# A hand-written order for the projection stage of an RWKV-7 layer

## The chip, the cores and the metric

The kernel runs on one NeuronCore of a Trainium2 chip. The core has five engines that run their own instruction streams in order: TensorE (PE, the matrix multiplications), VectorE (DVE), ScalarE (ACT), GpSimd (POOL) and SyncE (SP, which here issues every DMA). The metric is the device time of one execution in microseconds; the figure compared is the median over runs. One further execution is recorded by the profiler, and all durations below come from that one.

## The reference, cut to what matters

The model is a trunk of four layers over 512 latent tokens and 256 context tokens of width 1024: convolution, RWKV-7 time mixing, grouped-query attention, convolution. Each layer is modulated by vectors that are computed from a conditioning vector and a weight matrix. The change concerns the features of the second layer:

```python
def rwkv_features(h, proj, with_out):
    xx = centred_shift(h) - h
    lerp = lambda n: h + xx * mu[n]
    k = lerp(2) @ w_k
    v = heads(lerp(3) @ w_v)
    kk = heads(k * k_k)
    kk = kk * lax.rsqrt(jnp.sum(kk * kk, axis=-1, keepdims=True) + 1e-12)
    xw, xa = lerp(1), lerp(4)
    for d in range(2):
        w_log = -jax.nn.softplus(-(w0[d] + jnp.tanh(xw @ w1[d]) @ w2[d])) - 0.5
        a = jax.nn.sigmoid(a0[d] + (xa @ a1[d]) @ a2[d])
        ...  # decay exp(-exp(w_log)), k * (1 + (a - 1) * k_a), a
    r = heads(lerp(0) @ w_r)
    g = lerp(5) @ w_g
```

A recurrence over the tokens (the scan) then uses r, k, v, kk, a and the decay. `modulation(c, mod_w[i], mod_b[i])` is a product of a vector with a 1024 x 3072 matrix; the one of the last layer (i = 3) is computed inside this stage.

## The kernel before, in words

Tokens lie on the free axis, 768 of them with gaps of one between the two streams; channels lie on the 128 partitions in 8 tiles (`NT`). A projection of one column tile is the sum over 8 channel tiles. Each product is made of three matmuls in a split format: high weight by high input, high by low, low by high (`mm3`, L186), for 256 context and 512 latent tokens. These six matmuls are called a chunk here; a column tile has 8 chunks. The tile `pps` (for v `vps`) is a PSUM tile of two banks, and two of them exist.

The stage goes through these parts:

- The ramp (L743 on): for each channel tile m, `norm` (L676) makes the normed input H and the shifted difference XX on DVE and ACT; `mr.step` mixes the input for r (`mq`, then a high part `mh` and a low part `ml`); a low-rank product (`lps`, L746) reads H and XX.
- The r phase: 8 column tiles of `w_r`. Beside it run the low-rank product for the decay (`lora`, L775, on `mt`), the mixed input for the gate, which goes to DRAM (`dgx`), and the modulation of layer 3 (`mps` L205, `mrow`, `mpt` L212).
- The k phase: 8 column tiles of `w_k`, each with a follow-up: on ACT the copy out of PSUM (L834), kp and its square `ksq`; on PE the matmuls `pa` (L845) whose tanh gives the rate `ta`; `kd` and q on DVE; `pn` (L865) sums the squares, ACT copies them to `rn` and POOL takes the power -0.5 (L868); `pr` (L874) spreads that over the channels; kp, `ta` and `kh` are multiplied; `pb` (L887) sums q to `b`. Results go to DRAM as `dF` and `db`.
- The v phase: one column tile of `w_v` (`V_FIRST = 1`) in the stage, the other seven given as a generator to the scan, which places their chunks among its own work.

The first matmul of the scan is `pz` (L1017). It reads `RW`, small weights that are loaded into memory that the stage held before.

In this kernel, a scheduler with a simulated timeline orders the instructions of the stage on each engine; the scan behind it is written in its final order (`manual_schedule`). The modulation is advanced by two steps for every r tile and three for every k tile. Weight columns are loaded two tiles ahead on SP (L164), and ACT and DVE split them into `whi` and `wlo` (L173, L175).

Of the kernel before, what the change touches and what calls it, by code (L numbers as in the profile page):

```python
# [16 lines left out]
D = 1024  # L17
# [61 lines left out]
class Trunk:  # L79
# [582 lines left out]
    def rwkv_features(self, i, c1, cv):  # L662
# [5 lines left out]
        bank = lambda tag, name: ps_x.tile([P, 512], F32, tag=tag, name=name, bufs=2)  # L668
# [6 lines left out]
        def norm(m):  # L675
            for z in (0, CTX + 1, W - 1):  # L676
                nc.gpsimd.memset(H[m][:, z:z + 1], 0.0)
            for s, o, t0, n in segs:
                hs = H[m][:, 1 + o:1 + o + n]
                nc.vector.scalar_tensor_tensor(out=hs, in0=self.xs(m, s), scalar=self.gs[i][:, m, s:s + 1],  # L680
                                               in1=self.R[:, t0:t0 + n], op0=ALU.mult, op1=ALU.mult)
                nc.scalar.activation(hs, hs, AF.Identity, bias=self.shift_c(i, m, s))
            t = self.tp.tile([P, 783], F32, tag="sq", name="nb")
# [15 lines left out]
        def wcol(name, m):  # L699
            return self.wload(I[name][0][:, m * P:(m + 1) * P], NT, P, nc.vector)  # L700

        class Mix:

            def __init__(mx, n):
                mx.n, mx.h, mx.l = n, [], []

            def step(mx):
                k, n = len(mx.h), mx.n
                if k == NT:
                    return  # L710
# [10 lines left out]
        self.mp, self.mbufs = c1.enter_context(tc.tile_pool(name="mp1", bufs=1)), 2  # L721
        self.mod_ps = lambda: (bank("fill", "mps"), lambda: bank("fill", "mpt"))
        mod3 = self.modulation(DEPTH - 1, 256)
# [3 lines left out]
        lsegs = ((0, 0, CTX), (1, CTX + 1, SEQ))  # L727

# [5 lines left out]


        wa = lora_w("rwkv_a1")
        wm = fa.tile([P, NT, P], F32, tag="lw", name="lmu", bufs=2)
        nc.vector.tensor_tensor(out=wm, in0=wa, in1=mu[:, 4 * NT:5 * NT].unsqueeze(2).to_broadcast([P, NT, P]), op=ALU.mult)
        pl = [bank("fill", "lps") for _ in range(2)]
        ahead = [wcol("rwkv_w_r", m) for m in range(2)]  # L740
        for m in range(NT):
            norm(m)
            mr.step()  # L743
            for j, (w, x) in enumerate(((wa, H[m][:, 1:W - 1]), (wm, XX[m]))):
                for b, t0, n in lsegs:
                    nc.tensor.matmul(pl[b][:, :n], w[:, m, :], x[:, t0:t0 + n], start=m == 0 and j == 0, stop=m == NT - 1 and j == 1)  # L746
        for b, (_, t0, n) in zip(pl, psegs):
            nc.scalar.activation(AL[:, t0:t0 + n], b[:, :n], AF.Copy)
        self.rpool.close()
        self.xcpool.close()  # L750
        self.xpool.close()
        fp = c1.enter_context(tc.tile_pool(name="f1", bufs=1))
        self.mark("L1lora")

        def project(ws, x):

            pw = [(self.ps_b.tile([P, 1024], F32, tag="big", name="pps"), w) for w in ws]
            for k in range(NT):
                for ps, w in pw:
                    self.mm3([(ps[:, 0:CTX], slice(0, CTX)), (ps[:, 512:1024], slice(CTX + 1, CTX + 1 + SEQ))],  # L760
                             [a[:, k:k + 1] for a in w], ([x.h[k]], [x.l[k]]), 1, first=k == 0, last=k == NT - 1)
            return [ps for ps, _ in pw]

        def evac(dst, ps, f):
            for o, t0, n in psegs:
                f(dst[:, t0:t0 + n], ps[:, o:o + n], t0, n)

        def lora(n, name, done):

            wr = lora_w(name)  # L770
            ps = [bank("fill", "lps") for _ in range(2)]
            for k in range(NT):
                t = plain(n, k)
                for b, t0, n_ in lsegs:
                    nc.tensor.matmul(ps[b][:, :n_], wr[:, k, :], t[:, t0:t0 + n_], start=k == 0, stop=k == NT - 1)  # L775
                if k == NT - 1:
                    done(ps)
                if k % 2:
                    yield

        def phase(label, name, x, nxt, body, post, ahead):

            self.mark(label)
            done = []
            for m in range(NT):
                if not done:
                    n = 2 if m == 0 else 1
                    done = project([ahead.pop(0) for _ in range(n)], x)
                    for j in range(m + 2, min(m + 2 + n, NT)):
                        ahead.append(wcol(name, j))  # L790
                if m:
                    post(m - 1, prev)
                prev = body(m, done.pop(0))
                for _ in range(2):
                    next(fill, None)
                for _ in range(2 if x is mr else 3):
                    next(mod3, None)
                if nxt is not None:
                    nxt.step()
            return lambda: post(NT - 1, prev)  # L800

        def decay_done(ps):
            for b, (_, t0, n) in zip(ps, psegs):
                nc.scalar.activation(self.T[0][0:64, t0:t0 + n], b[0:64, :n], AF.Tanh)
                nc.scalar.activation(self.T[1][64:128, t0:t0 + n][:, ::-1], b[64:128, :n], AF.Tanh)

        def gate_lerp():

            for k in range(NT):
                nc.sync.dma_start(self.dgx[k], plain(5, k))  # L810
                yield

        def filler():
            yield from lora(1, "rwkv_w1", decay_done)
            yield from gate_lerp()

        fill = filler()

        def r_body(m, ps):
            r = self.tp.tile([P, TOK], F32, tag="t", name="r")  # L820
            evac(r, ps, lambda d, p, t0, n: nc.scalar.activation(d, p, AF.Copy))
            nc.sync.dma_start(self.dF[m][:, 1, :], r)

        last = phase("L1r", "rwkv_w_r", mr, mk, r_body, lambda m, st: None, ahead)
        ahead = [wcol("rwkv_w_k", 0), wcol("rwkv_w_k", 1)]
        A2 = fa.tile([P, NT, P], F32, tag="lw", name="A2", bufs=2)
        nc.sync.dma_start(A2, I["rwkv_a2"][0].rearrange("d l (m c) -> (d l) m c", c=P))


        def k_body(m, ps):  # L830
            r = fp.tile([P, TOK], F32, tag="f3", name="rl")
            nc.sync.dma_start(r, self.dF[m][:, 1, :])
            k = self.tp.tile([P, TOK], F32, tag="t", name="k")
            evac(k, ps, lambda d, p, t0, n: nc.scalar.activation(d, p, AF.Copy))  # L834
            kp = fp.tile([P, TOK], F32, tag="f0", name="kp")
            nc.scalar.activation(kp, k, AF.Copy, scale=self.vec("k_k")[:, m:m + 1])
            sq = self.tp.tile([P, TOK], F32, tag="sq", name="ksq")
            nc.scalar.activation(sq, kp, AF.Square)
            ta, kd = [], []
            for d in range(2):  # L840
                w = slice(64 * d, 64 * d + 64)
                t = fp.tile([P, TOK], F32, tag=f"ta{d}", name=f"ta{d}")
                for o, t0, n in psegs:
                    pa = bank("post", "pa")
                    nc.tensor.matmul(pa[:, :n], A2[w, m, :], AL[w, t0:t0 + n], start=True, stop=True)  # L845
                    nc.scalar.activation(t[:, t0:t0 + n], pa[:, :n], AF.Tanh, scale=0.5,
                                         bias=self.a0h[:, d * NT + m:d * NT + m + 1])
                ta.append(t)
                f = fp.tile([P, TOK], F32, tag="f1", name="kd", bufs=2)
                nc.scalar.activation(f, t, AF.Identity, scale=self.KA[:, 1, m:m + 1], bias=self.KA[:, 0, m:m + 1])  # L850
                nc.vector.tensor_tensor(out=f, in0=f, in1=k, op=ALU.mult)
                for sl, h in ((1, HA), (0, HB)):
                    nc.sync.dma_start(self.dF[m][h, 2 + 2 * d + sl, :], f[h])
                kd.append(f)
            q = fp.tile([P, TOK], F32, tag="f2", name="q")
            nc.vector.tensor_tensor(out=q, in0=kd[0], in1=kd[1], op=ALU.add)
            nc.vector.scalar_tensor_tensor(out=q, in0=q, scalar=self.vec("r_k")[:, m:m + 1], in1=r, op0=ALU.mult, op1=ALU.mult)
            return kp, sq, ta, q
# [1138 lines left out]
```

## Time and profile before

| | us |
|---|---|
| median of 3 runs | 2523.52 (2518.95 to 2536.96) |
| profiled execution | 2515.72 |
| its span, first to last instruction | 2513.9 |
| mean granted TensorE clock, as a share of the full one | 0.934 |
| PE busy over the span | 2317.8 (92%) |
| DVE, ACT, POOL busy | 1420.7, 1107.9, 513.7 |

The stage lies between about 432 and 774 us of the span. Times in the rows are microseconds from the start of the span, unless they are marked ns. The granted clock stands as a share of full speed. "Idle before" is the time that an engine waited in front of an instruction, with what ended the wait. An fp32 matmul shows up as two matmul records; those of the split format as one.

### The profile page before, as it was taken

The page shows a single profiled execution, that of the slowest core. Times are in us where ns is not written, and L with a number is a line of the kernel's source. Part 1 is how long each engine was busy: PE and PEld are TensorE (multiplying, and loading weights), DVE is VectorE, ACT ScalarE, POOL GpSimd, SP SyncE. Part 2 cuts the span into 40 slices and gives each one's busy share as a digit, 9 for nine tenths or more (in the row PEclk, how much of TensorE's full clock was granted, in tenths as well). Part 3 has the DMA queues.
Part 4 walks back from the last instruction along what each step waited for, and adds up shares of the span by engine and source line. Part 5 has one row for each costly group of instructions (what it writes and reads, how often), then busy time and mean ns, then how long its engine had stood idle before and what let it go on. Part 6 is the DMA issues. An engine that isn't in the chain of part 4 may idle for free. (4 is left out here: it accounts for less than half of the span.)

```text
span 2513.9 us, 45763 instructions
## 1 busy us (share of the span) xinstructions
PE 2317.8 (92%) x17983; PEld 1818.0 (72%) x17983; DVE 1420.7 (57%) x2565; ACT 1107.9 (44%) x2642; POOL 513.7 (20%) x600
## 2 busy tenths in 40 slices
PE   7999978999887889999999899989999999989987
PEld 4777757677656667777776677878988989865655
DVE  4856665643533766666664342745455464668774
ACT  4222243333542256666666643446445454442232
POOL 0000002000101123223220004445344454410000
PEclk9999989999888889899887899999999999999999
DMA  8877633267564554444432463111111211215442
GB/s 269 242 218 212 173 101 118 75 190 225 169 197 149 155 124 113 110 120 118 110 89 64 143 219 114 33 53 43 43 58 45 68 60 51 83 31 133 119 127 84
DMA packets 358997, 304.50 MB, mean 121 GB/s; under 512 B 110886, under 2 KB 300414, under 8 KB 358782
## 3 DMA queue, kind: packets, MB, share of 16 engines
q1 hardware_dynamic: 358782, 301.57, 41.5%
q8 instruction: 142, 2.33, 0.4%
q14 instruction: 73, 0.60, 0.1%
HBM read 215.82 MB, written 57.77 MB: 109 GB/s over the span
## 5 line engine op out<-in xcount | busy, mean ns | idle before, releaser
L173 ACT ACTIVATE whi<-wraw 128x1024 fp32r<-128x1024 f32 x168 | 177.0, 1056 | 408.7 <-PE cps L186 180.6
L175 POOL TENSOR_TENSOR wlo<-wraw,whi 128x1024 fp32r<-128x1024 f32 x70 | 168.2, 2406 | 183.0 <-ACT whi L173 170.2
L370 DVE SCALAR_TENSOR_TENSOR Y<-yp,VC,Y 128x783 f32<-128x783 f32 (+1 forms) x224 | 196.8, 891 | 8.1 <-ACT Y L363 4.2
L175 DVE TENSOR_TENSOR wlo<-wraw,whi 128x1024 fp32r<-128x1024 f32 x98 | 120.2, 1228 | 137.8 <-ACT whi L173 129.0
L1750 PE MATMUL pj<-whi,hhi 128*128 128x256 f32 x640 | 182.7, 286 | 5.2 <-ACT junk L1759 3.6
L1750 PE MATMUL pj<-wlo,hhi 128*128 128x256 f32 x640 | 182.2, 285 | 2.4 <-POOL wlo L175 2.4
L1750 PE MATMUL pj<-whi,hlo 128*128 128x256 f32 x640 | 181.9, 285 | 0.0
L186 PE MATMUL cps<-hhi,whi 128*128 128x512 f32 x576 | 178.9, 367 | 3.0 <-ACT hhi L285 3.0
L186 PE MATMUL cps<-hhi,wlo 128*128 128x512 f32 (+1 forms) x576 | 176.9, 361 | 0.0
L186 PE MATMUL cps<-hlo,whi 128*128 128x512 f32 (+1 forms) x576 | 176.5, 360 | 0.0
L186 PEld LDWEIGHTS cps<-hhi,whi 128*128 128x128 f32 x576 | 96.5, 190 | 47.4 <-issue 15.9
L1750 PEld LDWEIGHTS pj<-whi,hhi 128*128 128x128 f32 x640 | 123.7, 193 | 6.5 <-ACT junk L1759 4.2
L186 PE MATMUL ops<-hhi,whi 128*128 128x512 f32 (+1 forms) x320 | 104.9, 370 | 24.6 <-ACT hhi L445 22.2
L1750 PEld LDWEIGHTS pj<-wlo,hhi 128*128 128x128 f32 x640 | 123.9, 194 | 3.3 <-POOL wlo L175 2.6
L1750 PEld LDWEIGHTS pj<-whi,hlo 128*128 128x128 f32 x640 | 123.5, 193 | 0.1
L994 ACT ACTIVATE VT<-c 64x64 f32<-64x64 f32 x384 | 83.5, 218 | 82.9 <-PE c L1269 76.5
L1283 ACT ACTIVATE VT<-o,DC 64x64 f32<-64x64 f32 x352 | 108.8, 309 | 21.5 <-PE o L1278 12.7
L186 PEld LDWEIGHTS cps<-hhi,wlo 128*128 128x128 f32 x576 | 95.9, 189 | 25.9 <-issue 10.0
L186 PEld LDWEIGHTS cps<-hlo,whi 128*128 128x128 f32 x576 | 96.7, 190 | 22.7 <-issue 5.0
L1175 DVE TENSOR_TENSOR Ti<-Ti,tm 96x31 f32<-96x31 f32 (+15 forms) x248 | 105.8, 427 | 6.1 <-POOL tm L1172 0.2
L186 PE MATMUL ops<-hhi,wlo 128*128 128x512 f32 (+1 forms) x320 | 106.5, 363 | 3.0 <-POOL wlo L175 2.2
L186 PE MATMUL ops<-hlo,whi 128*128 128x512 f32 (+1 forms) x320 | 104.9, 356 | 0.5 <-DVE hlo L656 0.5
(343 smaller groups left out, 5806.1 us busy)
## 6 DMA issues: line engine op xcount, KB each, us to landing
mraw<-in_mod_w_dram SPq DMA_DIRECT2D x36, 1024.0 KB
wraw<-in_conv_w_in_dram SPq DMA_DIRECT2D x48, 512.0 KB
wraw<-in_attn_w_in_dram SPq DMA_DIRECT2D x48, 512.0 KB
X<-yp SPq DMA_DIRECT2D x128, 99.4 KB
mraw<-in_mod_w_dram SPq DMA_DIRECT2D x24, 512.0 KB
KR<-dF SPq DMA_DIRECT2D x24, 384.0 KB
F<-dF SPq DMA_DIRECT2D x24, 384.0 KB
X<-yp SPq DMA_DIRECT2D x128, 65.5 KB
```

Of the source, the lines that this page charges most:

```text
L173: nc.scalar.activation(hi[:, :n], raw[:, :n], AF.Copy)
L175: lo_eng.tensor_tensor(out=lo[:, :n], in0=raw[:, :n], in1=hi.bitcast(F32)[:, :n], op=ALU.subtract)
L186: nc.tensor.matmul(ps, a[:, k, m0:m0 + m], b[k0 + k][:, ts], start=first and k == 0 and i == 0, stop=last and k == kt - 1 and i == 2)
L370: taps.append(lambda v=v: nc.vector.scalar_tensor_tensor(out=Y[m], in0=y[:, PE_TAPS + v:PE_TAPS + v + nout], scalar=self.vec("dw", nv)[:, ...
L994: nc.scalar.activation(out, in_, AF.Copy)
L1175: eng("ia", j).tensor_tensor(out=Ti[0:96, j + 1:32, 0:c], in0=Ti[0:96, j + 1:32, 0:c], in1=o, op=ALU.add)
L1283: nc.scalar.activation(G["VT", h2][own, d, q2, hc(hd)], pS[own], AF.Copy, scale=dc[own])
L1750: nc.tensor.matmul(o[:, n, :], a, b[:, k, :], start=kh == 0 and k == 0 and e == 0 and n == 0, stop=kh == 1 and k == 3 and e == 2 and n == 1)
```

## The change

The stage is put under `manual_schedule`, so that PE, DVE, ACT and POOL run its instructions nearly in the order in which the code makes them; SP is still ordered by the scheduler. Column tiles go in pairs, the second 4 chunks behind the first (2 in the first pair of r). A small calendar (`at`, `tick`) places each piece of a key tile's follow-up a set number of chunks behind the tile's last chunk: rate at 0 and 1, norms at 2, kd at 3, the bonus at 4, spread and products at 5, the weighing at 6. The r chunks start inside the ramp. Of the 37 turns of the modulation, 28 come in the r phase and 9 in the k phase. Four PSUM banks are one pool for all helpers, in place of two pools of two. `kp` has two buffers, `b` moves to another buffer, and the rates of even tiles use buffers of the v phase.

```diff
-        bank = lambda tag, name: ps_x.tile([P, 512], F32, tag=tag, name=name, bufs=2)
+        bank = lambda name: ps_x.tile([P, 512], F32, tag="post", name=name, bufs=4)
...
+        def at(d, f):
+            plan.setdefault(now[0] + d, []).append(f)
+
+        def tick():
+            for f in plan.pop(now[0], []):
+                f()
+            now[0] += 1
...
+        def ready(j):
+            if j < len(cols):
+                ws[j] = self.wsplit(raws.pop(j), NT, P, nc.vector)
+                fetch(j + 2)
...
+            at(0, key)
+            at(0, lambda: rate(*psegs[0]))
+            at(1, lambda: rate(*psegs[1]))
+            at(2, norms)
+            at(3, lambda: kd(0))
+            at(3, lambda: kd(1))
+            at(4, bonus)
+            at(5, spread)
+            at(5, products)
+            at(6, weigh)
+
+        def phase(label, j0, x, nxt, body, beside, lead=lambda p: 4, before=lambda k: None):
+            self.mark(label)
+            for p in range(0, NT, 2):
+                ps, L = [big("pps") for _ in range(2)], lead(p)
+                steps = [(e, k) for u in range(NT + L) for e, k in ((0, u), (1, u - L)) if 0 <= k < NT]
+                for u, (e, k) in enumerate(steps):
+                    if e == 0 and p == 0:
+                        before(k + 1)
+                    chunk(ps[e], ws[j0 + p + e], x, k)
+                    if k == NT - 1:
+                        body(p + e, ps[e])
+                        at(0, lambda j=j0 + p + e + 2: ready(j))
+                    if p == NT - 2 and e == 1:
+                        nxt.step()
+                    beside(p // 2, u)
+                    tick()
+            nxt.step()
+
+        with ExitStack() as man:
+            man.enter_context(tc.manual_schedule(engines={nc.tensor.engine, nc.vector.engine, nc.scalar.engine, nc.gpsimd.engine}))
+            fetch(0)
+            fetch(1)
+            wa = lora_w("rwkv_a1")
+            wm = fa.tile([P, NT, P], F32, tag="lw", name="lmu", bufs=2)
+            ready(0)
+            nc.vector.tensor_tensor(out=wm, in0=wa, in1=mu[:, 4 * NT:5 * NT].unsqueeze(2).to_broadcast([P, NT, P]), op=ALU.mult)
...
+            def r_beside(p, u):
+                if u % 2 and (p or u > 7):
+                    next(mod3, None)
+                if p in (1, 2):
+                    if u % 2 == 0:
+                        next(decay, None)
+                    if u % 4 == 3:
+                        next(gate, None)
+
+            phase("L1r", 0, mr, mk, r_body, r_beside, lambda p: 4 if p else 2, ramp)
...
+            phase("L1k", NT, mk, mv, k_body, lambda p, u: next(mod3, None) if p < 3 and u in (6, 9, 12) else None)
...
+            for m in range(V_FIRST):
+                for _ in v_tile(m):
+                    tick()
+            while plan:
+                tick()
```

What this does to the instruction streams is shown at three places. The first is PE at the end of the stage, in front of the scan's first matmul `pz`. Before, behind the last of 24 v chunks:

```order
L186 MATMUL vps<-mh,wlo 128x512
L887 MATMUL pb<-q,C 128x512
L845 MATMUL pa<-AL,A_4453 128x256
L845 MATMUL pa<-AL,A_4453 128x512
L845 MATMUL pa<-AL,A_4453 128x256
L845 MATMUL pa<-AL,A_4453 128x512
L865 MATMUL pn<-blk_3529,ksq 128x2 x6
L874 MATMUL pr<-C,rn 64x128 x12
L887 MATMUL pb<-q,C 128x256
L887 MATMUL pb<-q,C 128x512
```

The same eight rows from `pa` to `pb` follow once more, for the last key tile, and then `pz`. In the changed kernel, the end of the last follow-up on PE:

```order
L891 MATMUL pr<-C,rn 64x128 x12
L186 MATMUL vps<-mh,whi 128x256
L186 MATMUL vps<-mh,whi 128x512
L186 MATMUL vps<-ml,whi 128x256
L186 MATMUL vps<-ml,whi 128x512
L186 MATMUL vps<-mh,wlo 128x256
L186 MATMUL vps<-mh,wlo 128x512
L909 MATMUL pb<-q,C 128x256
L909 MATMUL pb<-q,C 128x512
L186 MATMUL vps<-mh,whi 128x256
```

The follow-ups of the last two key tiles moved in front of the v chunks: behind the last `pb` now come 86 matmuls of v (14.3 chunks) and then `pz`. In both kernels 24 v chunks precede `pz`.

The second place is PE in the k phase, around the rates (`pa`) of a key tile. Before, the four matmuls of the rates of the fifth tile and its norms (`pn`) stand together, ahead of the first v chunk:

```order
L887 MATMUL pb<-q,C 128x512
L845 MATMUL pa<-AL,A_4453 128x256
L845 MATMUL pa<-AL,A_4453 128x512
L845 MATMUL pa<-AL,A_4453 128x256
L845 MATMUL pa<-AL,A_4453 128x512
L865 MATMUL pn<-blk_3529,ksq 128x2 x6
L186 MATMUL vps<-mh,whi 128x256
L186 MATMUL vps<-mh,whi 128x512
```

In the changed kernel, where the second tile of a pair has ended:

```order
L891 MATMUL pr<-C,rn 64x128 x12
L857 MATMUL pa<-AL,A_4532 128x256 x2
L186 MATMUL pps<-mh,whi 128x256
L186 MATMUL pps<-mh,whi 128x512
L186 MATMUL pps<-ml,whi 128x256
L186 MATMUL pps<-ml,whi 128x512
L186 MATMUL pps<-mh,wlo 128x256
L186 MATMUL pps<-mh,wlo 128x512
L909 MATMUL pb<-q,C 128x256
L909 MATMUL pb<-q,C 128x512
L857 MATMUL pa<-AL,A_4532 128x512 x2
```

The rates are split: the 256-wide ones come right at the tile's end, the 512-wide ones a chunk later, and the first tile's spread (`pr`) and weighing (`pb`) stand ahead of each; the norms follow another chunk later.

The third place is DVE at the start of the ramp. Before, with the 512-wide multiplies of all eight tiles ahead of the reciprocal for the context tokens (rows of the first three tiles left out):

```order
L680 SCALAR_TENSOR_TENSOR H_3557<-xl_86,gs_72,R 128x512
L680 SCALAR_TENSOR_TENSOR H_3558<-xl_87,gs_72,R 128x512
L680 SCALAR_TENSOR_TENSOR H_3559<-xl_88,gs_72,R 128x512
L680 SCALAR_TENSOR_TENSOR H_3560<-xl_89,gs_72,R 128x512
L680 SCALAR_TENSOR_TENSOR H_3561<-xl_90,gs_72,R 128x512
L260 RECIPROCAL R<-R 128x256
L175 TENSOR_TENSOR wlo<-wraw,whi 128x1024 x2
```

and in the changed kernel:

```order
L260 RECIPROCAL R<-R 128x256
L175 TENSOR_TENSOR wlo<-wraw,whi 128x1024
L951 TENSOR_TENSOR lmu<-lraw,VT 128x1024
L680 SCALAR_TENSOR_TENSOR H_3554<-xl_83,gs_72,R 128x512
L680 SCALAR_TENSOR_TENSOR H_3554<-xc_94,gs_72,R 128x256
L680 SCALAR_TENSOR_TENSOR H_3555<-xl_84,gs_72,R 128x512
L680 SCALAR_TENSOR_TENSOR H_3555<-xc_95,gs_72,R 128x256
L686 TENSOR_TENSOR nb<-H_3554 128x769
L687 SCALAR_TENSOR_TENSOR XX_3562<-nb,H_3554 128x769
L693 SCALAR_TENSOR_TENSOR mq<-XX_3562,VT,H_3554 128x769
```

The multiplies of H moved behind the reciprocal, one `wlo` and `lmu` (which stood earlier, in the layer before), and then go tile by tile with the rest of the ramp.

## Rows read from the trace of the kernel before

**Rows 1.** Windows by stretch: length, busy time by engine (instructions), PEclk, DMA share, GB/s
```profile
442.00:475.00 33.00, 30.86 (x104) 19.47 (x105) 33.00 (x42) 10.14 (x17) 0.00 (x0) 0.87 0.09 28
475.20:639.40 164.20, 164.20 (x997) 123.65 (x995) 62.77 (x78) 58.24 (x95) 4.83 (x2) 0.99 0.63 194
726.00:775.00 49.00, 26.83 (x104) 16.93 (x103) 16.07 (x19) 16.77 (x28) 6.51 (x7) 0.61 0.58 183
```

**Rows 2.** Timeline of PE, 740 to 774: start, length, instruction, idle before and releaser
```profile
740.74 2.83 PE L874 MATMUL pr<-C,rn 128*64 128x128 f32 x24 [3.37 <-POOL rn L868]
748.41 3.00 PE L845 MATMUL pa<-AL,A 64*128 64x256 f32 x6 [2.92 <-ACT b L888]
760.20 2.83 PE L874 MATMUL pr<-C,rn 128*64 128x128 f32 x24 [3.37 <-POOL rn L868]
773.90 1.62 PE L1017 MATMUL pz<-RW,T 128*128 128x128 f32 x6 [8.70 <-DMA RW<-in_rwkv_w_dram]
```

**Rows 3.** Groups of PE instructions, 639.4 to 773.8: count, busy, mean ns, idle before
```profile
L845 PE MATMUL pa<-AL,A 64*128 64x256 f32 (+1 forms) x40 | 20.0, 669 | 8.6 <-ACT b L888 6.1 <-ACT ta L846 2.6
L186 PE MATMUL vps<-ml,whi 128*128 128x256 f32 (+1 forms) x48 | 14.3, 374 | 0.0
L865 PE MATMUL pn<-blk,ksq 128*128 128x2 f32 x72 | 12.5, 302 | 0.6 <-ACT ta L846 0.6
L874 PE MATMUL pr<-C,rn 128*64 128x128 f32 x144 | 11.8, 326 | 6.7 <-POOL rn L868 6.7
L186 PE MATMUL pps<-mh,whi 128*128 128x256 f32 (+1 forms) x32 | 10.9, 429 | 2.3 <-ACT k L834 2.3
```

**Rows 4.** Windows for the tile pps alone, PE: length, busy (matmuls), PEclk
```profile
442.20:475.20 33.00, 9.72 (x40) 0.88 0.09 27
475.20:485.05 9.85, 9.85 (x57) 1.00 0.38 101
```

**Rows 5.** Timeline of PE, 541 to 655, at full clock
```profile
541.42 0.64 PE L205 MATMUL mps<-mraw,sc 128*32 128x256 f32 x8
547.90 0.64 PE L205 MATMUL mps<-mraw,sc 128*32 128x256 f32 x8
603.73 0.70 PE L845 MATMUL pa<-AL,A 64*128 64x256 f32 x2
604.91 1.12 PE L845 MATMUL pa<-AL,A 64*128 64x512 f32 x2
639.45 1.50 PE L865 MATMUL pn<-blk,ksq 128*128 128x2 f32 x12
649.14 1.53 PE L874 MATMUL pr<-C,rn 128*64 128x128 f32 x24
654.91 1.02 PE L887 MATMUL pb<-q,C 128*128 128x512 f32 x2
```

**Rows 6.** Timeline of DVE, 387 to 446
```profile
387.32 2.30 DVE L738 TENSOR_TENSOR lmu<-lraw,VT 128x1024 f32<-128x1024 f32 x1
432.65 4.72 DVE L680 SCALAR_TENSOR_TENSOR H<-xl,gs,R 128x512 f32<-128x512 f32 x7
438.95 2.29 DVE L175 TENSOR_TENSOR wlo<-wraw,whi 128x1024 fp32r<-128x1024 f32 x2
441.16 3.25 DVE L680 SCALAR_TENSOR_TENSOR H<-xc,gs,R 128x256 f32<-128x256 f32 x8
444.33 1.82 DVE L684 TENSOR_TENSOR nb<-H 128x769 f32<-128x769 f32 x2
```

**Rows 7.** Timeline of PE at 664, behind a wait
```profile
664.11 1.01 PE L186 MATMUL pps<-mh,whi 128*128 128x256 f32 x2 [2.31 <-ACT k L834]
668.12 0.82 PE L186 MATMUL pps<-mh,whi 128*128 128x256 f32 x2
```

**Rows 8.** Timeline of POOL at 662
```profile
662.39 2.88 POOL L868 TENSOR_TENSOR rn<-rn,mhalf 128x12 f32<-128x12 f32 x1 [17.99 <-ACT rn L867]
```

**Rows 9.** Timeline of DVE at 663
```profile
663.18 0.96 DVE L856 TENSOR_TENSOR q<-kd 128x768 f32<-128x768 f32 x1
```

More of the change, by code (lines that the diff above doesn't have):

```diff
@@ L673, in rwkv_features, with normed @@
         segs = [(0, CTX + 1, CTX, SEQ), (1, 0, 0, CTX)]
-        def norm(m):
+        def normed(m):
             for z in (0, CTX + 1, W - 1):
@@ L727, in rwkv_features, with fetch, chunk, evac @@
         lsegs = ((0, 0, CTX), (1, CTX + 1, SEQ))
+        big = lambda name: self.ps_b.tile([P, 1024], F32, tag="big", name=name)
+        plan, now = {}, [0]
+        def at(d, f):
[4 more added lines that the diff above has]
+            now[0] += 1
+        cols = [I[n][0][:, m * P:(m + 1) * P] for n in ("rwkv_w_r", "rwkv_w_k", "rwkv_w_v") for m in range(NT)]
+        raws, ws = {}, {}
+        def fetch(j):
+            if j < len(cols):
+                raws[j] = self.wfetch(cols[j], NT, P)
+        def ready(j):
+            if j < len(cols):
+                ws[j] = self.wsplit(raws.pop(j), NT, P, nc.vector)
+                fetch(j + 2)
+        def chunk(ps, w, x, k):
+            self.mm3([(ps[:, 0:CTX], slice(0, CTX)), (ps[:, 512:1024], slice(CTX + 1, CTX + 1 + SEQ))], [a[:, k:k + 1] for a in w],
+                     ([x.h[k]], [x.l[k]]), 1, first=k == 0, last=k == NT - 1)
+        def evac(dst, ps):
+            for o, t0, n in psegs:
+                nc.scalar.activation(dst[:, t0:t0 + n], ps[:, o:o + n], AF.Copy)
         def lora_w(name):
@@ L733, in lora_w @@
             return wr
[L736 to L744, printed above, removed]
-                for b, t0, n in lsegs:
-                    nc.tensor.matmul(pl[b][:, :n], w[:, m, :], x[:, t0:t0 + n], start=m == 0 and j == 0, stop=m == NT - 1 and j == 1)
@@ L747, in rwkv_features @@
[L747 to L800, printed above, removed]
@@ L803, in decay_done, with lora_decay @@
+        mod3 = modulation(DEPTH - 1)
+        def lora_decay():
+            wr = lora_w("rwkv_w1")
+            ps = [bank("lps") for _ in range(2)]
+            for k in range(NT):
+                t = plain(1, k)
+                yield
+                for b, t0, n in lsegs:
+                    nc.tensor.matmul(ps[b][:, :n], wr[:, k, :], t[:, t0:t0 + n], start=k == 0, stop=k == NT - 1)
+                yield
             for b, (_, t0, n) in zip(ps, psegs):
@@ L824, in rwkv_features @@
[L824 to L827, printed above, removed]
-        def k_body(m, ps):
[L831 to L846, printed above, removed]
-                                         bias=self.a0h[:, d * NT + m:d * NT + m + 1])
[L848 to L851, printed above, removed]
@@ new lines, in spread @@
+            def spread():
+                kp, rn = t["kp"], t["rn"]
+                for o, t0, n in psegs:
+                    pr = bank("pr")
+                    for u in range(n // P):
+                        c = t0 // P + u
+                        for e, h in enumerate((HA, HB)):
+                            nc.tensor.matmul(pr[h, u * P:u * P + P], rn[:, 2 * c + e:2 * c + e + 1].to_broadcast([P, 64]), self.ident,
+                                             start=True, stop=True)
+                    nc.vector.tensor_tensor(out=kp[:, t0:t0 + n], in0=pr[:, :n], in1=kp[:, t0:t0 + n], op=ALU.mult)
@@ new lines, in weigh @@
+            def weigh():
+                b = self.tp.tile([P, TOK], F32, tag="sq", name="b")
+                for o, t0, n in psegs:
+                    pb = bank("pb")
+                    nc.tensor.matmul(pb[:, :n], self.blk, t["q"][:, t0:t0 + n], start=True, stop=True)
+                    nc.scalar.activation(b[:, t0:t0 + n], pb[:, :n], AF.Copy)
+                nc.sync.dma_start(self.db[m], b)
+            at(0, key)
+            at(0, lambda: rate(*psegs[0]))
+            at(1, lambda: rate(*psegs[1]))
```

241 lines of the change are left out of this document (148 added, 93 removed).

## The prediction

> **What bounds the kernel now.** I read the stage in four steps. First the windows by stretch. In the ramp VectorE is busy for all of 33.0 us, so it sets the pace there. From 475.2 to 639.4 TensorE is busy for all of 164.2 us at a clock of 0.99, so nothing but less matmul work shortens that. From 726 to 775 TensorE is busy for 26.8 of 49.0 us at a clock of 0.61, and no other engine is busy for more than 17 us: that stretch is a chain of waits [rows 1]. Second the timeline of that stretch: two follow-ups run one behind the other, 19.5 us apart from `pr` to `pr`, each with 3.37 us of waiting for POOL's power, with up to 2.92 us for ACT, and then 8.70 us for a DMA in front of `pz` [rows 2]. Third the groups of TensorE from 639.4 to 773.8: they tell how much work is in those 134.4 us [rows 3]. Fourth single instructions at full clock, for the prices [rows 4, 5].
>
> **The work behind 639.4.** The tile pps alone, between 475.2 and 485.05, has 57 matmuls in 9.85 us, 0.173 us each, so a chunk of six costs 1.04 us [rows 4]. A follow-up at full clock: `pa` twice (0.70 + 1.12) = 3.64, `pn` 1.50, `pr` 1.53, `pb` 1.02 for its 512-wide part and, in the proportion of `pa`, 0.60 for the other (an estimate); 8.3 us in all [rows 5]. From 639.4 to 773.8 there are 24 v chunks (three kinds of 48 matmuls) and 16 key chunks (three kinds of 32), 41.6 us; five tiles' `pa` (40 records, 8 a tile), 18.2; six tiles' `pn` (72, 12 a tile), 9.0; six tiles' `pr` (144, 24 a tile), 9.2; six `pb`, 9.7; and a last piece of modulation, 1.5 [rows 3, 5]. That is 89.2 us, so 45.2 of the 134.4 us are waiting and half clock.
>
> **The change part by part.** (1) The follow-ups of the last tiles go in front of the v chunks. The matmul work stays, the 45.2 us are what the order can win. All 14.3 v chunks behind the last `pb` cover the load of `RW`: 14.9 us against the 8.70 us that `pz` waited with nothing in front of it; I take 0 for that wait, and 8.7 as its upper end [rows 2].
>
> (2) The ramp. VectorE's 512-wide multiplies of H, which ran from about 432 on, now stand behind one `wlo` and `lmu`. Two `wlo` ended at 441.2, so one ends at about 440 at the latest, and `lmu` adds 2.3. Per channel tile the rest is 4.72/7 + 3.25/8 for H and four passes over 769 columns at 0.9, together 4.7 us; eight tiles and the second `wlo` make 38.8 [rows 6]. With a start between 440.4 and 442.4, and the last three passes not needed for the low-rank product, that product ends at 477 to 481; before, it ended with the ramp at about 475. I take 478, 3 us later. In exchange 10 chunks of r stand ahead of its end, where before 40 matmuls, 6.7 chunks, did [rows 4]: 3.3 x 1.04 = 3.5 us less to do behind.
>
> (3) Behind the ramp TensorE has 164.2 + 89.2 - 3.5 = 249.9 us of work. From 478 that puts `pz` at 727.9 in place of 773.9: 46.0 us earlier, if it never waits.
>
> (4) New waits. At the end of the second tile of each pair ACT has `kh` of the first tile, the copy of the second, kp, its square and two tanh in its queue, and the four banks are then held by `pa` and `pb`: the 512-wide `pa` waits for the first tanh, with all later chunks behind it on TensorE. It occurs four times; the nearest row is `pa` waiting 2.92 us for ACT [rows 2], below it nothing. I take half, 1.45: 5.8 us. Behind a wait of 2.31 us six pairs of matmuls took 4.0 us, 0.67 each instead of 0.35, so 1.9 us more, since the clock had fallen [rows 7]. Four times 0 to 1.9; I take half, 3.8 us. The chunks on both sides speak for less than the whole.
>
> (5) Modulation. Its matmuls stay as they are; 18 of 24 weight blocks now come in the r phase, with their DMAs in SP's queue among the stores of r and of the gate's input. Hidden by r chunks: two successive uses of one buffer lie 6 chunks, a column group's 2 us and decay work apart, about 10 us; before, two such uses lay 6.5 us apart (541.42 and 547.90, with one other block between) and no wait stands at either [rows 5]. I take 0; without that cover each block would stop TensorE. In the k phase fewer loads remain beside the stores.
>
> (6) The second `kp` buffer, the moved `b`, the borrowed v buffers and the gate's two buffers take away waits of ACT and VectorE that TensorE did not wait for while it was dense: 0. The scan behind `pz` has the same order on TensorE as before: 0, and it starts earlier by what `pz` does.
>
> **A rule against it.** POOL's power of a tile (2.88 us) now falls where VectorE does kd and q. In the trace VectorE's q, which reads two operands from SBUF, starts 0.8 us inside such a power and takes 0.96 us [rows 8, 9]: neither stops the other for long. The Trainium skill, SBUF — State Buffer, section "SBUF: two separate sides", says that the pair of ports shared by VectorE and GpSimd is an exclusive lock for a whole instruction, against VectorE operations with two SBUF inputs as well; this row disagrees, since q ended long before the power did.
>
> **The sum.** 46.0 - 5.8 - 3.8 = 36.4 us. The profiled execution took 2515.72 us, 7.8 below the median; from it the sum gives 2479.3, and from the median of 2523.52, with which the result will be compared, 2487.1. I predict **2487 us**.
>
> **The rivals.** *A, slower:* in the written order TensorE stands still at each `mps` whose weight block has not landed, with r chunks behind it that could have run; the scheduler had placed blocks where it thought them loaded. With 24 blocks, 1.5 us of waiting at each eats the 36 us, and 2.6 us makes it slower by 1%; at 3 us the time is 2487 + 72 = 2559. For it: SP is one queue, and r stores now stand among the loads. Against it: the 6.5 us above, and 194 GB/s over the dense stretch without a wait [rows 1]. It decides from the point where a block needs more than the 10 us of its two turns.
>
> *B, no change:* the follow-ups pace the k phase, since one's chain is 19.5 us long [rows 2]. If the two of a pair do not overlap, a pair takes 39 us instead of 16 chunks and two follow-ups, 33.2; four pairs cost 23 us more: 2510. Against it: their starts lie only 5 chunks apart, and over the two chains of the last stretch ACT was busy for 16.8 us and VectorE for 16.1, so that both have room in 33 us [rows 1].
>
> *C, the lock:* if each of the eight powers stopped VectorE for 2.88 us and all of it reached TensorE, 23 us go: 2510. The Trainium skill's section above would have it so.
>
> *D, the change does not do what it says:* `pz` is held by something that does not move with TensorE's order, the 8.7 us of the `RW` load from a later release: 2496.
>
> **How the numbers follow.** Chances: the forecast 0.66, A 0.10, B 0.15, C 0.03, D 0.06. The forecast's own range goes from no new waits (2477.5, and 7 less because the runs before spread over 18 us) to whole waits, whole clock losses and the wait at `pz`, 46.0 - 11.7 - 7.6 - 8.7 = 18.0 us won, 2505.5. B and C reach 2510 and are taken in: 2470 to 2512. About 1% (25 us, below 2498 or above 2549) is what a measurement of this kernel can tell from no change. Faster: the forecast but for its upper end (0.60) and most of D, 0.65. Within 1%: B, C, the rest of the forecast and of D, half of A, 0.28. Slower: the worse half of A, 0.07.
>
> **What would show it.** Right: `pz` at about 735 to 740 us of the span; TensorE's clock at 0.95 or more from the ramp's end to there, with no stretch like 726 to 775; waits of `pa` for ACT of 1 to 3 us at the second tile of each pair; the low-rank product's end at about 478. Wrong: waits of `mps` for `mraw` (A), of `pr` for POOL in every tile (B), powers that stretch VectorE's kd and q (C), a wait at `pz` (D), or a scan that takes longer from `pz` on.

## The result, and the profile after

The changed kernel takes 2506.60 us (median of 10 runs, 2493.83 to 2514.91), the kernel before 2526.15 in the runs beside it (10 runs, 2516.28 to 2536.96): a ratio of 0.9915, with a 95% interval of 0.9887 to 0.9943, some 21 us. I had forecast 36.4 us less; the time lies inside the range and 20 us above the forecast. The forecast's own range ended at 2505.5, and it is the part taken in for the rivals B and C, up to 2512, that holds the measured time; as a gain, some 21 us against 18.0 or more, it lies within the forecast's own. The profiled execution has a span of 2494.1 us against 2513.9, so 19.8 us less, and a mean clock of 0.949 against 0.934.

The windows of the changed kernel that answer to [rows 1]: the ramp, from the low-rank product's end to `pz`, from `pz` to `pc` (the scan's second product, which reads `sg`), and the 5.6 us behind it.

```profile
444.00:483.00 39.00, 36.06 (x124) 22.67 (x123) 36.48 (x45) 14.96 (x23) 0.00 (x0) 0.90 0.05 14
483.16:745.07 261.91, 244.12 (x1509) 182.25 (x1508) 123.26 (x149) 113.00 (x185) 19.52 (x13) 0.97 0.66 202
745.07:757.39 12.32, 1.88 (x14) 1.47 (x12) 3.32 (x4) 2.17 (x4) 0.00 (x0) 0.66 0.55 180
757.39:763.00 5.61, 5.61 (x20) 5.03 (x21) 0.17 (x1) 0.87 (x2) 1.91 (x3) 0.52 0.44 154
```

The stretch of 49 us in which TensorE was busy for only 27 [rows 1] is gone: from 483.2 to `pz` it is busy for 244.1 of 261.9 us. But behind `pz` a new hole of 10 us stands, and half clock after it (granted 0.52). On TensorE, answering to [rows 2]:

```profile
725.94 1.53 PE L891 MATMUL pr<-C,rn 128*64 128x128 f32 x24
745.07 0.83 PE L1112 MATMUL pz<-RW,T 128*128 128x128 f32 x6
746.44 0.51 PE L186 MATMUL vps<-mh,wlo 128*128 128x256 f32 x2
757.39 1.65 PE L1122 MATMUL pc<-C,sg 128*128 128x128 f32 x6 [10.44 <-DVE sg L1118]
```

`pz` waits for nothing and comes 28.8 us earlier than at 773.90 [rows 2]. `pc` came at 777.24 before and comes at 757.39: 19.9 us earlier. A third of the gain is lost between the two. VectorE and ScalarE show why:

```profile
747.95 0.96 DVE L1009 TENSOR_TENSOR b<-b,v 128x768 f32<-128x768 f32 x1 [9.23 <-DMA RW<-in_rwkv_w_dram]
748.83 1.22 DVE L175 TENSOR_TENSOR wlo<-wraw,whi 128x1024 fp32r<-128x1024 f32 x1
749.75 0.50 ACT L1116 ACTIVATE sg<-pz 128x384 f32<-128x384 f32 x1
756.11 0.96 DVE L1009 TENSOR_TENSOR b<-b,v 128x768 f32<-128x768 f32 x1 [6.06 <-DMA b<-db]
756.98 0.35 DVE L1118 TENSOR_SCALAR sg<-sg 128x384 f32<-128x384 f32 x1
```

and SP's issues of the same time:

```profile
740.86 0.97 SPq L1005 DMA_DIRECT2D b<-db  x1
748.94 0.37 SPq L1010 DMA_DIRECT2D dbv<-b  x1
751.26 0.32 SPq L1005 DMA_DIRECT2D b<-db  x1
```

`sg` needs 0.35 us of VectorE, and ScalarE had its tanh done at 750.3. It stands in VectorE's queue behind the products b*v of the second and third v tile. All v tiles share one buffer `b`: the product of one must be stored (748.94) before the b of the next is loaded (751.26), and VectorE waits for that load until 756.1. In the kernel before, the products of the same three tiles ran among the follow-ups:

```profile
703.75 0.95 DVE L910 TENSOR_TENSOR b<-b,v 128x768 f32<-128x768 f32 x1
717.47 0.95 DVE L910 TENSOR_TENSOR b<-b,v 128x768 f32<-128x768 f32 x1
729.48 0.96 DVE L910 TENSOR_TENSOR b<-b,v 128x768 f32<-128x768 f32 x1 [1.15 <-ACT v L908]
```

They stood 12 to 14 us apart there, and the last was done 43 us ahead of `pz`. Now the v tiles fill the stretch ahead of `pz`, one right behind the other, 8 chunks (some 8.3 us) each, and their products came along: the first runs at 734.06, and the store and reload of `b` put the next two 13.9 and 8.2 us later, behind `pz`. (In front of the product at 747.95 the profile names a load of `RW`; but that product reads only `b` and v, and v was copied by 738.5.)

### The profile page after: what moved, and what is told of

It is laid out like the page before. It is cut to its first block, busy times and chain, and to the rows that moved or that the text cites. A ratio compares the mean times of both kernels' runs of the same rounds, so it can differ in the third digit from the quotient of the medians.

```text
span 2494.1 us, 45739 instructions
## 1 busy us (share of the span) xinstructions
PE 2292.1 (92%) x17983; PEld 1793.2 (72%) x17983; DVE 1415.8 (57%) x2565; ACT 1104.9 (44%) x2642; POOL 510.9 (20%) x600
## 5 line engine op out<-in xcount | busy, mean ns | idle before, releaser
L380 PE MATMUL yps<-X,W 128*32 128x512 f32 (+1 forms) x768 | 103.1, 525 | 3.7 <-DMA X<-yp 3.7
```

The costliest lines, as they stand in the source:

```text
L380: nc.tensor.matmul(p[32 * c:32 * c + 32, 512 * s:512 * s + n], W[m][:, q, c, :], X[m][:, c, o + 4 * q:o + 4 * q + n], start=q == 0, stop=q ...
```

## The experiments

All twelve compare with the kernel before. A single profile's `pz` moves by several us with the granted clock, so idle time of TensorE, which repeats (17.5 to 17.8 us in the changed kernel, e1, e3 and e7), stands beside it. The ratios carry the clock too: e7 is 18 us slower than the changed kernel by the ratios and 7.7 us by the way from start to `pc`. "Start" is the last `ops` matmul of the layer before; "idle" is TensorE's from the end of the low-rank product to `pz`; all three columns are in us.

| kernel | ratio to before (95%) | start to `pz` | idle | `pz` to `pc` |
|---|---|---|---|---|
| before | 1 | 342.9 | 29.1 | 3.3 |
| changed | 0.9915 (0.9887 to 0.9943) | 312.2 | 17.8 | 12.3 |
| e1 no product | 0.9842 (0.9815 to 0.9869) | 311.0 | 17.5 | 4.2 |
| e2 b apart | 0.9864 (0.9840 to 0.9889) | 316.7 | 18.6 | 1.9 |
| e3 split early | 0.9930 (0.9907 to 0.9953) | 322.7 | 17.5 | 12.4 |
| e4 rates later | 0.9866 (0.9841 to 0.9890) | 306.1 | 13.8 | 12.6 |
| e5 split later | 0.9951 (0.9917 to 0.9985) | 323.6 | 21.8 | 7.2 |
| e6 no v mix | one run, 2503.20 us | 303.0 | 11.5 | 11.8 |
| e7 no ramp chunks | 0.9988 (0.9956 to 1.0021) | 320.9 | 17.5 | 11.3 |
| e8 modulation in k | 0.9972 (0.9948 to 0.9996) | 320.7 | 22.0 | 7.0 |
| e9 last uncovered | 0.9908 (0.9874 to 0.9942) | 317.0 | 25.6 | 3.2 |
| e10 one by one | 0.9869 (0.9828 to 0.9909) | 309.6 | 11.9 | 5.8 |
| e11 combined | 0.9860 (0.9821 to 0.9899) | 303.9 | 14.8 | 1.9 |
| e12 combined, lead 2 | 0.9867 (0.9825 to 0.9909) | 308.4 | 15.8 | 3.3 |

### The hole behind `pz`: e1 and e2

```diff
-                b = self.vt.tile([P, TOK], F32, tag="b", name="b")
-                nc.sync.dma_start(b, self.db[m])
...
-                nc.vector.tensor_tensor(out=b, in0=b, in1=v, op=ALU.mult)
-                nc.sync.dma_start(self.dbv[m], b)
+                nc.sync.dma_start(self.dbv[m], v)
```

> Leaves out the product of b and v and the load of b: the v tile is stored in its place, so the bonus term is not the reference's. Theory 1 (the queue): behind `pz`, VectorE's scaling of `sg` stands behind two products b*v, each of which waits for the one buffer b to go to DRAM and come back; `pc` waits 10.44 us for it. Without the products `pc` starts within 3 us of `pz` (wait below 1 us), no half clock follows, and the scan's milestones come 10 to 13 us earlier than in the changed kernel: about 2494 us against 2506.6. Theory 2 (the loads): the scan's first features wait for the loads of KR, F and RW that SP issues between 738 and 762; then `pc` comes earlier, but a wait of 5 us or more appears at the first `pg`, and the time stays within 3 us of 2506.6.

`pc` waits 2.3 us in place of 10.4 (below 1 was expected), no half clock follows (clock 1.00 from 745 to 800), `pc` comes 9.4 us earlier against the start, and the time falls by 18 us against the changed kernel by the ratios, 9 by the spans. The ratio holds more than this one wait, since e1 leaves out the load and the product of every v tile, in the scan too. The whole computation with the products out of `sg`'s way:

```diff
-                b = self.vt.tile([P, TOK], F32, tag="b", name="b")
+                b = (self.vt if m else self.tp).tile([P, TOK], F32, tag="b" if m else "sq", name="b")
...
+                    if k == 2 and owed:
+                        owed.pop()()
...
+                def product():
+                    nc.vector.tensor_tensor(out=b, in0=b, in1=v, op=ALU.mult)
+                    nc.sync.dma_start(self.dbv[m], b)
+                if 0 < m < NT - 1:
+                    owed.append(product)
+                else:
+                    product()
```

> Keeps the whole computation. The first v tile's b goes to another buffer, and the product of each later v tile is put two chunks into the next tile, behind the scan's `sg`. Theory 1 (the queue): the wait at `pc` falls from 10.44 us to below 2 us, no half clock follows it, and the time falls by 8 to 12 us, to about 2497 (ratio to the kernel before about 0.988). Theory 2 (the loads): a new wait of 5 us or more at the next features (`pg`, or `pc` again) and a time within 3 us of 2506.6. Theory 3 (the product only moves): VectorE waits for the load of b in the next `pz`/`pc` pair instead, and half of the gain is lost: 2501.

TensorE in e2:

```profile
749.62 0.91 PE L1122 MATMUL pz<-RW,T 128*128 128x128 f32 x6 [1.04 <-issue]
751.56 0.94 PE L1132 MATMUL pc<-C,sg 128*128 128x128 f32 x6
```

No wait is left at `pc`, and none of 5 us appears behind it (the longest there is 0.6 at `pg`). Theory 1 holds, theories 2 and 3 fall. The ratio is 0.005 lower, 13 us, though the two intervals still touch; this profile's own span (2496.3) shows no gain, since it had a lower clock from 720 to 745 (0.88 against 1.00) and in the scan.

### The ramp: e3 and e7

```diff
                 if k + 1 < NT:
                     normed(k + 1)
+                if k == 0:
+                    raw = raws.pop(1)
+                    hi = self.wp.tile([P, 1024], F32R, tag="whi", name="whi")
+                    nc.scalar.activation(hi, raw, AF.Copy)
...
                 mr.step()
                 if k == 0:
-                    ready(1)
+                    lo = self.wp.tile([P, 1024], F32R, tag="wlo", name="wlo")
+                    nc.vector.tensor_tensor(out=lo, in0=raw, in1=hi.bitcast(F32), op=ALU.subtract)
...
```

> In the ramp, ScalarE makes the second tile's whi ahead of the mh it stood behind, and VectorE its wlo one pass later, so that VectorE's wait of 1.92 us in front of that wlo goes. Theory 1: VectorE paces the ramp, so the low-rank product ends about 1.9 us earlier than 482.6 and `pz` comes 1.5 to 2 us earlier. Theory 2: TensorE paces the ramp (36.1 of 39.0 us busy from 444 to 483), so the end moves by less than 0.7 us. Either is below what the times can tell; the trace decides.

The last group of the low-rank product starts 46.7 us behind the start in place of 48.8: 2.1 us earlier, as theory 1 has it; e11 and e12, which hold the same edit, have 46.7 too. That `pz` is later in this profile has another cause, shown below.

```diff
+            for j in range(1, NT + 1):
+                ramp(j)
-            phase("L1r", 0, mr, mk, r_body, r_beside, lambda p: 4 if p else 2, ramp)
+            phase("L1r", 0, mr, mk, r_body, r_beside, lambda p: 4 if p else 2)
```

> The r chunks wait for the end of the ramp. Theory 1 (the prediction's step 2): VectorE paces the ramp with or without chunks, so the low-rank product ends at 480 to 482 as before, and the 10 chunks of 1.04 us go behind it: `pz` 9 to 10 us later, time about 2515 against 2506.6. Theory 2: TensorE paces the ramp (36.1 of 39.0 us busy); without the chunks the product ends 4 us or more earlier, and `pz` is less than 6 us later.

Without chunks beside it the product ends only 0.9 us earlier, and TensorE has 9.9 us more to do behind it (busy 254.0 against 244.1 us, idle the same 17.5). Theory 1: VectorE paces the ramp, and a chunk inside it is free.

### Rates, and the last pair: e4, e5, e6

```diff
+            z = m % 2
...
-            at(1, lambda: rate(*psegs[1]))
-            at(2, norms)
+            at(1 + z, lambda: rate(*psegs[1]))
+            at(2 + z, norms)
```

(and so on, to `weigh` at 6 + z)

> For the second tile of each pair the 512-wide rates and all pieces behind them come one chunk later. Theory 1: the four waits of `pa` for ScalarE (8.1 us, 1.8 to 2.15 each) are covered by the chunk of 1.04 us and shrink to 0.7 to 1.1 each, 4 to 4.4 us less, and with the clock that holds `pz` comes 4 to 6 us earlier. Theory 2: the bank is free only when ScalarE gets there and the wait stays or moves to `pn` or `pr`: less than 2 us at `pz`. At the end `pc` still waits for the products, so of a gain at `pz` only a part reaches the time.

The four waits are 3.5 us together in place of 8.1, the longest 1.1, and idle falls by 4.0: theory 1. The ratio is lower by more than that, 0.9866, with an interval that touches the changed kernel's.

```diff
-                        at(0, lambda j=j0 + p + e + 2: ready(j))
+                        at(2 if j0 else 0, lambda j=j0 + p + e + 2: ready(j))
```

> In the k phase the split of the next weights (whi on ScalarE, wlo on VectorE) comes two chunks later. Theory 1 (VectorE's queue): in the last pair the chain is wlo waiting 4.38 us for whi, with the mixing of v's input queued behind it; mh, the rates and POOL's power come late through it, and TensorE waits 4.15 us at `pr`, 2.56 at `pb` and 1.76 at `pa` and falls to half clock. With wlo later, `pr`'s wait falls below 1.5 us, the three together below 4, and `pz` comes 5 to 9 us earlier than 745.1. Theory 2 (work, not order): 8 mixing steps of 2 us of VectorE and 0.85 of ScalarE stand in about 16 chunks, the last four in four chunks; the wait at `pr` stays above 3 us whatever the order of wlo, and `pz` moves by less than 2 us. `pc` still waits about 10 us in both, so the time falls by 4 us at most or stays.

```profile
710.16 1.53 PE L891 MATMUL pr<-C,rn 128*64 128x128 f32 x24 [0.57 <-POOL rn L869]
720.58 2.93 PE L909 MATMUL pb<-q,C 128*128 128x256 f32 x4 [6.99 <-DVE kp L893]
725.02 1.49 PE L857 MATMUL pa<-AL,A 64*128 64x512 f32 x4 [1.50 <-ACT ta L859]
```

The wait leaves `pr` and comes back at `pb`: 9.1 us for the three in place of 8.5. Theory 1 is wrong: the order of `wlo` only chooses where TensorE waits. Theory 2 is right in kind, but it named `pr` as the place, and `pz` comes 11.4 us later against the start where it allowed 2 (idle grows by 4.0).

```diff
         mk, mv, mr = (Mix(n) for n in (2, 3, 0))
+        mv.h, mv.l, mv.step = mk.h, mk.l, lambda: None
```

> Leaves out the mixing of v's input: the v phase multiplies with k's input. Upper end for the last pair: by theories 1 and 2 alike the waits of 4.15, 2.56 and 1.76 us at `pr`, `pb` and `pa` there vanish (below 1.5 us together beside the `pa` wait that every pair has) and TensorE keeps its clock from 690 to 720, so `pz` comes 10 to 14 us earlier, at 731 to 735. If they stay, neither the mixing nor what queues behind wlo makes them.

The waits at `pr` and `pb` are gone, `pa`'s 2.15 stays as in every pair, idle falls by 6.3 and `pz` comes 9.2 us earlier against the start, a little less than expected. So the mixing of v's input, eight times 2 us of VectorE in the last pair, is what TensorE waits for there. It can't be earlier: its output takes the buffers of k's input, which the last pair still reads.

### Where the pieces stand: e8, e9, e10

```diff
-                if u % 2 and (p or u > 7):
+                if u % 4 == 3 and (p or u > 7):
...
-... next(mod3, None) if p < 3 and u in (6, 9, 12) else None)
+... next(mod3, None) if p < 3 and u % 2 else None)
```

> Of the 37 turns of the modulation 14 come in the r phase and 23 in the first three pairs of the k phase, nearly the share of the kernel before (16 and 21), with all else as in the changed kernel. Theory 1 (the prediction's step 5): where they stand costs nothing; `pz` within 3 us of 745 and the time within the measurement. Theory 2: beside the follow-ups their copies (mrow) and adds (modT) stand in the queues of ScalarE and VectorE in front of rates and products; waits of `mpt` or `pa` grow by 0.5 us at each of 10 turns or more, and `pz` comes 5 to 10 us later.

```profile
570.50 1.01 PE L795 MATMUL mpt<-pick,mrow 128*128 128x2 f32 x4 [6.75 <-ACT mrow L791]
```

Idle grows by 4.2 us, but not by 0.5 at each turn: one `mpt` at the change from r to k waits 6.75 us (2.3 in the changed kernel), since its copy stands on ScalarE behind the r tile, a split and the decay's tanh with a table load of 1.28 us. The ratio, 0.9972, lies 0.0057 (14 us) above the changed kernel's, more than this wait explains; what the rest is stays open. Neither theory fits; the move was worth something, and the one place that this profile shows is that wait.

```diff
+            z = 16 if m == NT - 1 else 0
             at(0, key)
-            at(0, lambda: rate(*psegs[0]))
+            at(z, lambda: rate(*psegs[0]))
```

(and z added to all later pieces)

> The follow-up of the last key tile, but for its copies, stands behind the first v tile with no chunk between its pieces; the other 16 v chunks come behind it. It undoes the tail's new order for one tile of two. Theory 1 (the prediction's step 1): the chain is uncovered; it took 19.5 us in the kernel before, with 8.3 us of matmul work in it at full clock, so `pz` comes 8 to 14 us later against the stage's start (324 us behind the last `ops` matmul, not 312), with waits at `pr` (3 us, POOL), `pa` and `pb`. Theory 2: TensorE was going to wait in the last pair anyway, and what is lost behind is won there (4.2, 2.6 and 1.8 us of waits in the changed kernel): less than 4 us.

TensorE, and SP's issues:

```profile
737.19 1.46 PE L909 MATMUL pb<-q,C 128*128 128x256 f32 x4
749.63 1.62 PE L1113 MATMUL pz<-RW,T 128*128 128x128 f32 x6 [10.98 <-DMA RW<-in_rwkv_w_dram]
752.82 0.83 PE L1123 MATMUL pc<-C,sg 128*128 128x128 f32 x6
```
```profile
740.54 0.33 SPq L911 DMA_DIRECT2D db<-b  x1
745.93 0.26 SPq L1104 DMA_DIRECT2D RW<-in_rwkv_w_dram  x1
```

Against what was expected, the v chunks came to stand between the last follow-up's pieces, and none behind them. So the chain was covered, and what shows is the other thing: the loads of `RW` are released 5 us behind the last store of `b`, and `pz` waits 10.98 us for them, as it waited 8.70 before [rows 2]. `pz` is 4.8 us later, but `pc` follows it in 3.2 us, 4.3 earlier than in the changed kernel, and the time is the same. The chunks behind the last follow-up hide the load of `RW`; they gained nothing for the scan as long as `pc` waited for the b of the v tiles.

```diff
-... next(mod3, None) if p < 3 and u in (6, 9, 12) else None)
+... next(mod3, None) if p < 3 and u in (6, 9, 12) else None, lambda p: 8)
```

> In the k phase the column tiles come one behind the other (the second 8 chunks behind the first, not 4); the calendar of the follow-ups stays. Theory 1: a follow-up fits into the next tile's 8 chunks, its pieces lying 6 chunks apart, so that three of the four `pa` waits (2.1 us each) go, while in the last tile 8 mixing steps of 2 us VectorE stand in 8 chunks, 8 us more of waiting there: `pz` within 6 us of the changed kernel's 312 us behind the last `ops` matmul. Theory 2 (the prediction's rival B): a follow-up is too long for 8 chunks; `pr` waits 3 us for POOL in each tile and `pz` comes 20 us or more later.

`pr` waits once (3.9 us) and `pn` once (3.7), both in the last pair and not in each tile; three `pa` waits sum to 0.7, and idle is 11.9, 5.9 less. Theory 1 holds, and rival B is wrong even without pairs. In time it is not to be told from the changed kernel (0.9869, touching intervals), so no gain from the pairs is shown.

### The edits together: e11 and e12

e11 is e2, e3 and e4 in one. e12 has one line more:

```diff
-... if p < 3 and u in (6, 9, 12) else None)
+... if p < 3 and u in (6, 9, 12) else None, lambda p: 4 if p < NT - 2 else 2)
```

> The edits of e2 (b apart), e3 (split early) and e4 (rates later) together; the computation is whole. If they add up, `pz` comes 6 to 8 us earlier against the last `ops` matmul than the changed kernel's 312, and `pc` 3 us behind it instead of 12: about 306 and 309 against 312 and 324.5, 15 us less. Against the kernel before a ratio of about 0.985 (the changed kernel 0.9915). If e4's gain is only that the time at `pc` was to be waited for anyway, no more than e2's 0.9864 comes.

> As e11, and in the last pair of the k phase the second tile runs 2 chunks behind the first, not 4, so that six of the eight mixing steps of v's input have two chunks each instead of four. Theory 1: ScalarE and VectorE keep up longer, the waits at `pr` (4.2 us) and `pb` (2.6) fall to below 3 together, and `pz` comes another 3 to 6 us earlier than in e11. Theory 2: the two last follow-ups now stand 3 chunks apart, hold the four banks at once, and the waits only move to `pa` and `pn`: no gain, or up to 5 us lost.

```profile
734.88 0.91 PE L1130 MATMUL pz<-RW,T 128*128 128x128 f32 x6 [1.00 <-DMA dbv<-b]
736.81 0.94 PE L1140 MATMUL pc<-C,sg 128*128 128x128 f32 x6
```

In e11 `pz` comes 303.9 and `pc` 305.8 us behind the start, 18.7 less than the changed kernel's 324.5; the span is 2472.2 against 2494.1, the ratio 0.9860 and the median 2488.21 us. It has the lowest ratio of the whole kernels here, though its interval still overlaps the changed kernel's by 0.001. That its parts add up in time is not shown: e2 alone has 0.9864. In e12 the waits at `pr` and `pb` fall to 1.1 us together, but others come (`vps` 2.3, `pn` 1.1), and `pz` waits 4.1 us for `RW`: no gain, as theory 2 has it.

## Why the prediction was right in sign and too large

The profiles lie 19.8 us apart, 16.6 less than the 36.4 of the sum. By its steps:

**(6), the step that failed: the scan behind `pz` at 0.** It cost 9.0 us (`pz` to `pc` 12.3 against 3.3), and it is the last of the signs of being wrong that the prediction lists. I had looked at TensorE's order behind `pz`, which is unchanged, and not at what VectorE's queue holds there; e1 and e2 take the wait away.

**(2), the ramp.** The product's last matmul started at 482.6 and ended at 483.2, not 478: 1.9 us of it is a later start of the stage, 3.3 the ramp itself. Answering to [rows 6], from 441 on VectorE stands still once, in front of the second `wlo`, which I had priced at its busy time alone:

```profile
448.18 1.22 DVE L175 TENSOR_TENSOR wlo<-wraw,whi 128x1024 fp32r<-128x1024 f32 x1 [1.92 <-ACT whi L173]
```

e3 won 2.1 us there. The passes of a channel tile also took 4.85 us (454.17 to 459.02), not 4.7, which makes 1.2 over eight tiles. e7 shows that the step was right in kind.

**(3), the work: 14.6 us too much.** The groups of `pa` from 475 to 774 before, then of the changed kernel from 482 to 745:

```profile
L845 PE MATMUL pa<-AL,A 64*128 64x512 f32 x32 | 21.3, 750 | 3.0 <-ACT ta L846 1.9 <-ACT b L888 1.2
L845 PE MATMUL pa<-AL,A 64*128 64x256 f32 x32 | 12.7, 481 | 5.6 <-ACT b L888 4.9 <-ACT ta L846 0.7
```
```profile
L857 PE MATMUL pa<-AL,A 64*128 64x512 f32 x32 | 11.4, 703 | 8.1 <-ACT ta L859 8.1
L857 PE MATMUL pa<-AL,A 64*128 64x256 f32 x32 | 6.1, 463 | 0.0
```

The same 64 records took 34.0 us and now take 17.5. The timeline, beside [rows 5]:

```profile
586.70 0.70 PE L857 MATMUL pa<-AL,A 64*128 64x256 f32 x4
588.58 1.13 PE L857 MATMUL pa<-AL,A 64*128 64x512 f32 x4
```

Four records, both directions, in the 0.70 us that two took. The order rows that I showed had the two directions back to back, and I priced them one by one: 0.70 + 1.12 for eight tiles is 14.6 us. The Trainium skill, TensorE: Matmul & The Clock Gate, section "Part 3: Packing small matmuls — row/col tiling", says that matmuls whose contractions lie in different row groups of the array run at the same time. Here the two directions sit on partitions 0 to 63 and 64 to 127, and the rows agree. In e10, at a granted clock of 1.00, both cases stand beside each other:

```profile
601.44 1.13 PE L857 MATMUL pa<-AL,A 64*128 64x512 f32 x4
617.06 1.12 PE L857 MATMUL pa<-AL,A 64*128 64x512 f32 x2
618.41 1.12 PE L857 MATMUL pa<-AL,A 64*128 64x512 f32 x2 [0.23 <-ACT ta L859]
```

Where the second direction waited for a tanh, the two ran one behind the other, and each took the full 1.12 us. No run undoes it for all tiles, so the sum of 16.5 us is read from the profiles alone.

**(4), new waits: 17.8 us, not 5.8.** The waits of TensorE from 425 to 760:

```profile
PE pa L857 <- ACT ta L859: 8.1, 4, 2.1
PE pr L891 <- POOL rn L869: 4.2, 1, 4.2
PE pb L909 <- DVE kp L893: 2.6, 1, 2.6
PE mpt L795 <- ACT mrow L791: 2.3, 1, 2.3
```

Those at `pa` are where I put them, 8.1 for 5.8. The others I did not name. Those at `pr` and `pb` are the last pair's; its chain on DVE, ACT and TensorE:

```profile
692.04 1.22 DVE L175 TENSOR_TENSOR wlo<-wraw,whi 128x1024 fp32r<-128x1024 f32 x1 [4.38 <-ACT whi L173]
694.29 0.85 ACT L712 ACTIVATE mh<-mq 128x769 fp32r<-128x769 f32 x1 [2.28 <-DVE mq L693]
695.04 1.25 ACT L859 ACTIVATE ta<-pa,a0h 128x512 f32<-128x512 f32 x2
700.23 1.80 PE L891 MATMUL pr<-C,rn 128*64 128x128 f32 x24 [4.15 <-POOL rn L869]
```

e5 and e6 show that the mixing as such makes it. With 244.1 us busy, and 249.9 - 14.6 = 235.3 of work, 8.8 us are left for half clock and for the error of my other prices, where I had 3.8; from 690 to 720 the granted clock was 0.77, and 0.94 in e6, where the waits at `pr` and `pb` are gone. The balance: 1.9 + 3.3 + 9.0 + 12.0 - 14.6 + 5.0 = 16.6 us. Two errors of 12 and 15 us went against each other; without the gain that I did not see, some 5 us would have been left, which the interval can hardly tell from nothing. To that extent it is luck that the time fell into the range.

**(1), the tail.** No wait at `pz`, as predicted. But the gain from the tail's order was smaller than the 45.2 us of waiting and half clock that I gave it: TensorE's idle time up to `pz` fell from 29.1 to 17.8 us, and its busy time by 25.5, of which the rates alone are 16.5 and the chunks that moved into the ramp some 3.5. No run undoes this order alone: e9, which was to do it, left the chain covered. `pz` came at 745.1, not at 735 to 740.

**(5), the modulation,** was not worth 0: with it back in the k phase e8 is slower. **A** did not come: no `mps` waits for `mraw`. **B** fell by e10, **D** in the changed kernel, where `pz` does not wait. **C**, the lock: a pass of VectorE inside the power and one outside,

```profile
697.30 2.88 POOL L869 TENSOR_TENSOR rn<-rn,mhalf 128x12 f32<-128x12 f32 x1 [19.82 <-ACT rn L868]
```
```profile
696.04 0.95 DVE L716 TENSOR_TENSOR ml<-mq,mh 128x769 fp32r<-128x769 f32 x1
697.97 0.97 DVE L716 TENSOR_TENSOR ml<-mq,mh 128x769 fp32r<-128x769 f32 x1
```

take 0.95 and 0.97 us, though both inputs lie in SBUF: no stop, as in [rows 8, 9], against the rule weighed there.

## What to carry to other kernels

When work moves to fill a hole, list what moves with it, on every in-order queue and every single buffer, and follow it to its new place: here the v tiles brought along a product that loads, multiplies and stores through one buffer, and it ended up in front of the scan's critical 0.35 us. Price matmuls by the pairs in which the new order puts them, not one by one. And compare kernels of a few us by idle time and waits, which repeat, before comparing the moment at which something starts.

## What the hardware showed beside it

The same wait has two prices. The first `pa` wait is 2.07 us in the changed kernel and in e3, where nothing differs behind the ramp. In the changed kernel TensorE goes on at full clock (granted 1.00 from 604.06 to 609.85):

```profile
602.64 1.49 PE L857 MATMUL pa<-AL,A 64*128 64x512 f32 x4 [2.07 <-ACT ta L859]
604.06 0.63 PE L186 MATMUL pps<-mh,whi 128*128 128x256 f32 x2
604.53 0.52 PE L186 MATMUL pps<-ml,whi 128*128 128x256 f32 x2
```

and in e3 at half, until 614.4 (granted 0.52 from 604.63 to 614.89):

```profile
603.05 1.65 PE L857 MATMUL pa<-AL,A 64*128 64x512 f32 x4 [2.07 <-ACT ta L859]
604.63 1.01 PE L186 MATMUL pps<-mh,whi 128*128 128x256 f32 x2
605.44 0.84 PE L186 MATMUL pps<-ml,whi 128*128 128x256 f32 x2
```

From `pa`'s end to `pr` the same work takes 10.3 us (604.63 to 614.89) against 5.8 (604.06 to 609.85): 4.5 us for one wait, where I had allowed 0 to 1.9. Over the whole stretch to `pz` e3 has the same idle time (17.5 and 17.8 us) and 257.1 us busy against 244.1, at a clock of 0.92 against 0.97: 13 us from the clock alone. What decides it is not settled here.
